# Where the moving operands of a two-block transformer step start: inner activations moved to byte 192 of 256, other inputs to byte 128

## The chip, the cores and the metric

The program runs on one core of a Trainium2 chip, in one launch. The metric is the device time in microseconds, the median of several runs.

## The reference

256 tokens of 1024 features, with 256 tokens of context, go through two blocks of two layers each. All matrices are fp32.

- First block, for each of two layers: a half feed-forward, an attention (differential in the first layer, grouped with norms of queries and keys in the second) and another half feed-forward. Each has a modulated norm ahead of it, `rmsnorm(h) * (1 + scale) + shift`, and joins the stream as `h + gate * rmsnorm(y)`. A feed-forward is `(silu(x Wg) * (x Wu)) Wout`, 1024 to 2816 to 1024. The context's stream goes along until the second layer's attention; the last feed-forward has the 256 tokens alone.
- Second block, for each of two layers: one wide projection of `rmsnorm(x)` feeds a sparse attention over 64 chosen keys, a stick-breaking attention and a matrix memory. Each of the three results is gated, projected by `w_branch` and weighted by a sigmoid of further columns of the projection. Their sum goes through `w_out` onto the stream. A last norm ends the program.

## The kernel before

**Products.** Features lie on the 128 partitions and tokens along the free axis: 512 tokens (latent and context) or 256. An fp32 value is kept as two exact parts, high and low, of type fp32r. `unit` makes the parts of a weight tile, `wh` on ScalarE (L60) and `wl` on VectorE (L61), from a raw tile that `load` (L52) brings over SP's queue. `mm3` (L75) does three products for one k-tile of 128 features: `wh` with the input's high part (L78), `wh` with its low part (L79), `wl` with its high part (L80). In each the weights (128 columns) are the stationary operand, and the input is the moving one, 512 or 256 columns wide. TensorE runs them one behind the other in the program's order, and loads the next weights while a product runs.

**Inputs.** A sublayer's input x has 8 tiles of high parts, `xh0` to `xh7`, and 8 of low parts, from `new_x` (L265). In a feed-forward `psg` holds the products of `w_in` with x. The inner activations are split into `gh` and `gl` (L320, L321), tiles of the pool `slot`, and `psy` holds the products of `w_out` with them (`wout`, L347). With a `done` and two halves of tokens, the last pass of `wout` takes its last four columns one half of the tokens after the other, 256 wide. The attentions keep their outputs for `wout` in `slot` too (`oh`, `ol`, `ohl`), as well as the grouped attention's keys (`gkh`, `gkl`). In the second block `pair` (L792) does two units of 128 columns into one bank `psp`, 256 wide, from x or from a branch's parts `bh`, `bl`.

**Places.** A pool's tiles are given addresses in the order in which the pools are opened (`run`, L1354). The weights' pool `w`, the constants, `h` and `tmp` stay through both blocks. In bytes from the start of a partition, as the allocator gives them out for the kernel before:

| pool | starts at | byte in 256 | holds |
|---|---|---|---|
| `w` | 51,648 | 192 | `wh`, `wl`, 512 bytes for a k-tile |
| `x` | 84,416 | 192 | `xh`, `xl` of the first block, 2,048 bytes each |
| `yq` | 117,184 | 192 | y, queries, keys |
| `slot` | 195,200 | 128 | 16 tiles of 2,048 bytes: `gh`, `gl`, `oh`, `ol`, `ohl`, `gkh`, `gkl` and others |
| `x2` | 128,672 | 160 | `xh`, `xl` of the second block, 1,024 bytes each |
| `y2` | 145,056 | 160 | the second block's other tiles of 512 columns, `bh` and `bl` among them |

A half of the tokens begins 1,024 bytes into its tile, and every tile here is a multiple of 256 bytes long, so all moving operands of a pool start at the same byte in 256.

**Order.** In the first block the steps that make the modulation's vectors (`psada`) and other small work are dealt out between the units. In the second block the attentions' steps and the projections that don't depend on them alternate. Loads wait on SP's queue until their raw tile is free: three raw tiles in the first block, two in the second. `w` holds four units.

Of the kernel before, what the change touches and what calls it, by code (L numbers as in the profile page):

```python
# [4 lines left out]
F32 = mybir.dt.float32  # L5
# [7 lines left out]
KC = 8  # L13
DFF = 2816
EPS = 1e-6
LAMBDA_INIT = 0.8 - 0.6
# Tiles of one tag take their slots in the order of the program: streams that may overtake each other have tags of their own.
PSUM_TAGS = ({"p": 2, "s": 2, "a": 2, "o": 1, "f": 1}, {"p": 2, "s": 2, "a": 1, "b": 3})
PSUM_OF = {}         # name -> tags taken in turn, for the first and for the second block
# [13 lines left out]
# the other partition of a pair that is rotated: neighbours, and eight apart  # L33
# [10 lines left out]
class Block:  # L44
# [25 lines left out]
    def behind(self, ins, prev):  # L70
        """issue order alone: ins after prev on their engine"""
        self.tc.add_manual_dep(ins.ins, prev.ins.name,
                               mybir.DependencyInfo(mybir.DependencyClass.NoSync, mybir.DependencyReason.DATA), reason="order")
# [8 lines left out]
    def split(self, hi, lo, src):  # L82
        """src (SBUF or PSUM, fp32) -> hi, lo"""
        self.nc.scalar.copy(hi, src)
        self.nc.vector.tensor_sub(lo, src, hi.bitcast(F32))

# [1 line left out]
    def setup(self):  # L88
# [7 lines left out]
        # condition vectors, silu; a stationary block of 32 columns for each k-tile begins with its two  # L96
# [11 lines left out]
        # rows of 128 features -> columns  # L108
# [11 lines left out]
    def vecs(self, aps, name):  # L120
        """list of [r, 128] DRAM rows -> one [128, sum r] SBUF tile"""
# [19 lines left out]
    def adaln(self, i, blocks, tiles="adaw", ahead=2):  # L141
        """blocks of 512 columns of the modulation, evenly spaced, as a list of steps; a step's loads come ahead of its products"""
# [3 lines left out]
        nm = 4 // nj            # k-tiles in a step: four products side by side in the array's columns  # L146
# [46 lines left out]
    def gtab(self, i, kind, k, out=None, cs=slice(0, 8)):  # L193
        """per-feature scale tables, [128, 8, 2]"""
# [13 lines left out]
    def rstd_rows(self, acc, n=256, mean=1.0 / D):  # L208
        """acc [128, n]: partial sums of squares over partitions -> 1/rms on every partition, in PSUM [128, n]"""
# [11 lines left out]
    def spread(self, rs):  # L221
        """columns of token scalars -> one row on every partition, in PSUM"""
# [8 lines left out]
    def sumsq(self, src_of, hf, tag, eng=None, pin=False):  # L231
        """sum over chunks of src^2 (SBUF) for a half -> acc [128, 256]"""
# [14 lines left out]
    def pre_norm(self, hf, G, mT, k, R=None):  # L247
        """x = split(rmsnorm(h) * G + B), this half"""
# [16 lines left out]
    def new_x(self, n=512):  # L265
        self.xh = [self.xp.tile([128, n], F32R, name=f"xh{c}", tag=f"xh{c}") for c in range(KC)]
        self.xl = [self.xp.tile([128, n], F32R, name=f"xl{c}", tag=f"xl{c}") for c in range(KC)]
# [5 lines left out]
    def ffn_units(self, i, f, c):  # L273
        """gate and up columns c, then those of c + 1"""
        w = self.I['ffn_w_in'][i, f]
        raws = [self.load(w[:, o + c * 128:o + c * 128 + 256], 8, 256) for o in (0, DFF)]
        return [self.unit(raw, 8, j * 128) for j in range(2) for raw in raws]

    def ffn(self, i, f, halves, done, fill=(), then=None, mid=None):
# [3 lines left out]
        if len(halves) == 2:  # L283
            self.new_y()
        else:
            self.y = self.h[1]      # the context's stream has ended
        # places for the fill: after each pair of w_in units, after each pair of w_out columns of all but the last pass
        self.set_fill(fill, DFF // 128 + 4 * (len(PASSES) - 1))
        for pi, (p0, p1) in enumerate(PASSES):
            nk = p1 - p0  # L290
            gh, gl = {}, {}
            for c in range(p0, p1, 2):
# [5 lines left out]
                if c == 0:  # L298
                    for hf, s in [(0, slice(0, width))] if mid else [(hf, HALF[hf]) for hf in halves]:
                        if hf:  # L300
                            self.step_tail(9)
                        # the last chunks unit by unit: the first units give up their place sooner
# [7 lines left out]
                for j in range(2):  # L310
# [9 lines left out]
                    a = self.sp.tile([128, 512], F32R, name="gh", tag="slot")  # L320
                    b = self.sp.tile([128, 512], F32R, name="gl", tag="slot")  # L321
# [10 lines left out]
    def warm(self, func):  # L332
        """have the table of a function loaded before it is needed"""
# [3 lines left out]
    def place(self):  # L337
        """a place in the program for steps of other work"""
# [8 lines left out]
    def wout(self, w, oh, ol, halves, first, done=None):  # L347
        """y (+)= w^T o; with done, the last columns come for one half of the tokens after the other"""
# [64 lines left out]
    def proj(self, ps, w, xs, sls, nk=8):  # L413
        """ps[:, sl] = w^T x[:, sl] for each slice, k inner"""
# [17 lines left out]
    def rope(self, x, n, other, cs):  # L432
        """x [128, n*256] in SBUF, rotated in place; cs [128, 2, 256]"""
# [15 lines left out]
    def rsqrt(self, ss, n, mean, name, eps=EPS):  # L449
        """(ss * mean + eps) ** -0.5 for a few columns"""  # L450
# [8 lines left out]
    def da(self, done):  # L459
# [10 lines left out]
        # -lambda on every partition  # L470
# [22 lines left out]
        def front(h):  # L493
            """projections of one head, in steps"""
# [52 lines left out]
    def da_qk(self, ps, name, scale, cs, out):  # L547
        """q or k of a head: rotated where the tokens are latent ones, split; the rotation is left to the caller's moment"""
# [12 lines left out]
    def vtok(self, vT, v):  # L561
        """v^T -> v with tokens on partitions, [128, 4*128]"""
# [63 lines left out]
    def ga(self, done):  # L626
# [15 lines left out]
        def q_pair(ps):  # L642
            """two heads: gain, rotation, split; 1 / rms apart"""
# [7 lines left out]
            def rest():  # L651
# [3 lines left out]
                rq = self.rsqrt(pss[:, 0:4], 4, 1.0, "q", 128.0 * EPS)      # with the scores' 128 ** -0.5  # L655
# [4 lines left out]
        # queries first: the context's half of x is still on its way  # L660
# [22 lines left out]
        # keys and values of all tokens  # L683
# [108 lines left out]
    def pair(self, raw, nk=8, x=None, c0=0):  # L792
        """two 128-column units of raw -> one bank [128, 2*256]"""
# [8 lines left out]
    def silu_gate(self, ps, name):  # L802
        """2 * silu(ps)"""
# [13 lines left out]
    def small_units(self, l):  # L817
        """weights of the narrow projections in two units, spread over the rows where they are needed;
        what the other rows of the product hold is of no use, but their columns are there"""
# [8 lines left out]
    def hybrid(self, l):  # L828
# [4 lines left out]
        # projections that the sparse attention needs first  # L833
# [74 lines left out]
        # up-projections of the keys, transposed, 16 zero rows in front of each head  # L908
# [11 lines left out]
        for cp in range(2):  # L920
            qa = {}
            ps = [self.pst("psqa") for e in range(2)]      # the two halves of the rows write different banks
# [9 lines left out]
            ol = [self.t2("olat") for c in range(2)]       # heads 4cp, 4cp+1 | 4cp+2, 4cp+3  # L932
# [65 lines left out]
        accs = self.hc          # the context's stream has ended  # L998
# [40 lines left out]
    def index_bias(self, t, iq, ik, iw, sc):  # L1039
        """0 where a key is among the 64 chosen for the query, -1e30 elsewhere"""  # L1040
# [23 lines left out]
    def tok_rows(self, src, dst_of, n=2):  # L1064
        """two banks of [128 features x 2, 256 tokens] -> tokens on partitions; src: list of SBUF tiles [128, 512]"""
# [67 lines left out]
    def ml_proj(self, l, qk, va):  # L1133
        """projections for the matrix memory, as a list of steps"""
# [29 lines left out]
    def mlstm(self, l, ig, fg, qk, va, more):  # L1164
        nc = self.nc
        # gates, one head on each of four partitions
# [7 lines left out]
        nc.vector.scalar_tensor_tensor(ex, fg, 0.0, ex, ALU.min, ALU.subtract)      # log sigmoid(f)  # L1174
# [64 lines left out]
    def final(self):  # L1239
        """out = h g / rms(h), tokens on partitions: there 1 / rms is a scalar of each partition"""  # L1240
# [51 lines left out]
    def low(self, xl, t, B, xh):  # L1292
        """t + B less its high part; t is spent."""
# [3 lines left out]
    def first_block(self):  # L1297
# [3 lines left out]
        # the first shift and scale come in two parts, and the first products need only the first of them  # L1301
# [26 lines left out]
        def steep(i, g):  # L1328
            """the first steps of a group wait for the boundary"""
# [24 lines left out]
    def run(self):  # L1354
        tc, nc, I = self.tc, self.nc, self.I
        from contextlib import ExitStack
        with ExitStack() as es:
# [6 lines left out]
            with ExitStack() as e1:  # L1364
# [6 lines left out]
                self.gp = pool("gt", 3, e1)  # L1371
                self.sp = pool("slot", 16, e1)
                self.setup()
                self.first_block()
            with ExitStack() as e2:
# [4 lines left out]
                self.small = pool("small", 1, e2)  # L1380
                self.xp = pool("x2", 1, e2)
# [48 lines left out]
class Join:  # L1430
    """A sublayer's output y joins the stream, h' = h + G y / rms(y), and the next sublayer's input follows from it,
    x = h' G' / rms(h') + B, for one half of the tokens at a time.
    Both means of squares are ready together: sum h'^2 = sum h^2 + 2 r sum h G y + r^2 sum (G y)^2, r = 1 / rms(y).
    post, pre: (layer, first modulation chunk)"""
# [18 lines left out]
    def stream(self):  # L1453
        """sum of h^2"""
# [7 lines left out]
    def chunk(self, hf, c):  # L1462
        """sums over the chunks of features of y^2, h G y and (G y)^2, tokens along the free axis"""
# [12 lines left out]
        if c == KC - 1:  # L1476
            b.hold = (last, add, 4, 4)      # the fourth of the next units of weights comes behind

    def finish(self, hf):
        """in parts: other products come between them"""  # L1480
# [134 lines left out]
```

## Time and profile before

| | |
|---|---|
| median of 3 runs | 2602.63 us (2601.14 to 2602.85) |
| span of the profiled execution, first to last instruction | 2598.3 us |
| median less that span | 4.3 us |
| TensorE busy | 2500.7 us (96%) |
| mean granted clock of TensorE | 0.984 of full |
| VectorE, ScalarE, GpSimd busy | 55%, 40%, 16% |

The profiled execution has no time of its own besides its span. In the profile PE is TensorE, PEld its loading of weights, DVE VectorE, ACT ScalarE, POOL GpSimd and SP the engine whose queue issues most transfers. A product is listed with its start and a duration that reaches past the start of the next, so the distance between starts is not the duration. A name is that of a tile in the program; L78 is line 78.

### The profile page before, as it was taken

The page shows a single profiled execution, that of the slowest core. Times are in us where ns is not written, and L with a number is a line of the kernel's source. Part 1 is how long each engine was busy: PE and PEld are TensorE (multiplying, and loading weights), DVE is VectorE, ACT ScalarE, POOL GpSimd, SP SyncE. Part 2 cuts the span into 40 slices and gives each one's busy share as a digit, 9 for nine tenths or more (in the row PEclk, how much of TensorE's full clock was granted, in tenths as well). Part 3 has the DMA queues.
Part 4 walks back from the last instruction along what each step waited for, and adds up shares of the span by engine and source line. Part 5 has one row for each costly group of instructions (what it writes and reads, how often), then busy time and mean ns, then how long its engine had stood idle before and what let it go on. Part 6 is the DMA issues. An engine that isn't in the chain of part 4 may idle for free. (4 is left out here: it accounts for less than half of the span.)

```text
span 2598.3 us, 38082 instructions
## 1 busy us (share of the span) xinstructions
PE 2500.7 (96%) x15175; PEld 2105.4 (81%) x15175; DVE 1435.2 (55%) x2492; ACT 1038.1 (40%) x1740; POOL 406.3 (16%) x427
## 2 busy tenths in 40 slices
PE   7999999999999999999999999999989999899998
PEld 3777778666678888788888887799887999788998
DVE  4333337666565333474333477656785765676755
ACT  3222234554353222343222355644444544446443
POOL 1000016220051000150000153400330010201010
PEclk9999998999999999999999999999999999999999
DMA  8443423344432322243332243455533356433453
GB/s 282 153 154 129 147 97 99 126 148 150 149 116 86 107 97 97 98 146 114 114 101 94 98 155 125 143 182 180 161 105 113 106 158 194 140 98 114 138 187 130
DMA packets 321789, 346.56 MB, mean 133 GB/s; under 512 B 23906, under 2 KB 282568, under 8 KB 321612
## 3 DMA queue, kind: packets, MB, share of 16 engines
q1 hardware_dynamic: 320706, 343.35, 40.9%
q8 instruction: 119, 1.95, 0.3%
q10 hardware_dynamic: 906, 0.78, 0.1%
q14 instruction: 58, 0.48, 0.1%
HBM read 343.04 MB, written 1.05 MB: 132 GB/s over the span
## 5 line engine op out<-in xcount | busy, mean ns | idle before, releaser
L60 ACT CAST wh<-raw 128x1024 fp32r<-128x1024 f32 (+2 forms) x534 | 527.8, 998 | 1120.7 <-PE psg L79 554.1
L61 DVE TENSOR_TENSOR wl<-raw,wh 128x1024 fp32r<-128x1024 f32 (+2 forms) x534 | 639.4, 1203 | 549.0 <-ACT wh L60 547.0
L79 PE MATMUL psg<-xl,wh 128*128 128x512 f32 (+1 forms) x1472 | 523.6, 356 | 3.1 <-POOL xl L1295 3.0
L78 PE MATMUL psg<-xh,wh 128*128 128x512 f32 (+1 forms) x1472 | 523.3, 357 | 2.9 <-ACT xh L1322 2.3
L80 PE MATMUL psg<-xh,wl 128*128 128x512 f32 (+1 forms) x1472 | 521.4, 355 | 0.0
L78 PE MATMUL psp<-xh,wh 128*128 128x256 f32 x1248 | 357.2, 287 | 10.0 <-DVE mlu L1156 3.8
L80 PE MATMUL psp<-xh,wl 128*128 128x256 f32 x1248 | 354.5, 284 | 3.1 <-DVE wl L61 3.1
L79 PE MATMUL psp<-xl,wh 128*128 128x256 f32 x1248 | 356.7, 286 | 0.6 <-POOL xl L855 0.6
L78 PEld LDWEIGHTS psg<-xh,wh 128*128 128x128 f32 x1472 | 277.3, 189 | 59.0 <-ACT wh L60 12.6
L79 PEld LDWEIGHTS psg<-xl,wh 128*128 128x128 f32 x1472 | 278.2, 189 | 53.1 <-issue 8.1
L80 PEld LDWEIGHTS psg<-xh,wl 128*128 128x128 f32 x1472 | 278.0, 189 | 39.7 <-issue 0.8
L79 PE MATMUL psy<-gl,wh 128*128 128x512 f32 (+1 forms) x800 | 273.8, 342 | 2.6 <-DVE gl L323 2.5
L78 PE MATMUL psy<-gh,wh 128*128 128x512 f32 (+1 forms) x800 | 275.2, 344 | 0.0
L80 PE MATMUL psy<-gh,wl 128*128 128x512 f32 (+1 forms) x800 | 273.6, 342 | 0.0
L78 PEld LDWEIGHTS psp<-xh,wh 128*128 128x128 f32 x1248 | 237.3, 190 | 16.3 <-issue 5.7
L80 PEld LDWEIGHTS psp<-xh,wl 128*128 128x128 f32 x1248 | 237.6, 191 | 5.4 <-DVE wl L61 4.1
L79 PEld LDWEIGHTS psp<-xl,wh 128*128 128x128 f32 x1248 | 237.9, 191 | 4.1 <-issue 2.4
L243 POOL TENSOR_TENSOR acc<-acc,sq 128x256 f32<-128x256 f32 x70 | 56.9, 816 | 1108.2 <-ACT acc L237 1102.5
L319 DVE TENSOR_TENSOR g<-sg,psg 128x512 f32<-128x512 f32 (+1 forms) x88 | 54.5, 620 | 223.4 <-PE psg L80 223.4
L78 PEld LDWEIGHTS psy<-gh,wh 128*128 128x128 f32 x800 | 150.3, 188 | 26.4 <-ACT wh L60 5.0
L79 PEld LDWEIGHTS psy<-gl,wh 128*128 128x128 f32 x800 | 151.1, 189 | 22.7 <-DVE gl L323 3.2
L80 PEld LDWEIGHTS psy<-gh,wl 128*128 128x128 f32 x800 | 150.5, 188 | 21.6 <-issue 1.7
(473 smaller groups left out, 3651.6 us busy)
## 6 DMA issues: line engine op xcount, KB each, us to landing
raw<-in_ffn_w_in SPq DMA_DIRECT2D x88, 1024.0 KB
raw<-in_w_in SPq DMA_DIRECT2D x70, 1024.0 KB
adaw<-in_ada_w SPq DMA_DIRECT2D x240, 256.0 KB
raw<-in_ffn_w_out SPq DMA_DIRECT2D x32, 1024.0 KB
adas<-in_ada_w SPq DMA_DIRECT2D x48, 256.0 KB
raw<-in_ffn_w_out SPq DMA_DIRECT2D x16, 768.0 KB
raw<-in_da_w_in SPq DMA_DIRECT2D x12, 1024.0 KB
raw<-in_w_branch SPq DMA_DIRECT2D x24, 512.0 KB
```

The costliest lines, as they stand in the source:

```text
L60: a = nc.scalar.copy(wh[:, 0:nk, :], r)
L61: b = nc.vector.tensor_sub(wl[:, 0:nk, :], r, wh[:, 0:nk, :].bitcast(F32))
L78: mm(ps, lhsT=wh[:, k, :], rhs=xh, start=first, stop=False)
L79: mm(ps, lhsT=wh[:, k, :], rhs=xl, start=False, stop=False)
L80: mm(ps, lhsT=wl[:, k, :], rhs=xh, start=False, stop=last)
L243: b = (eng or nc.vector).tensor_tensor(acc, acc, sq, ALU.add)
L319: nc.vector.tensor_mul(g[:, 0:width], sg[:, 0:width], pu[:, 0:width])
```

## The change

Four edits move tiles within their partition. No instruction, transfer or wait is added or taken away. Comments and docstrings are gone too.

```diff
-    def new_x(self, n=512):
-        self.xh = [self.xp.tile([128, n], F32R, name=f"xh{c}", tag=f"xh{c}") for c in range(KC)]
-        self.xl = [self.xp.tile([128, n], F32R, name=f"xl{c}", tag=f"xl{c}") for c in range(KC)]
+    def new_x(self, n=512, at=0):
+        self.xh = [self.xp.tile([128, at + n], F32R, name=f"xh{c}", tag=f"xh{c}")[:, at:at + n] for c in range(KC)]
+        self.xl = [self.xp.tile([128, at + n], F32R, name=f"xl{c}", tag=f"xl{c}")[:, at:at + n] for c in range(KC)]
...
-                    a = self.sp.tile([128, 512], F32R, name="gh", tag="slot")
-                    b = self.sp.tile([128, 512], F32R, name="gl", tag="slot")
+                    at = 0 if width == 512 else 48
+                    a = self.sp.tile([128, 512], F32R, name="gh", tag="slot")[:, at:at + width]
+                    b = self.sp.tile([128, 512], F32R, name="gl", tag="slot")[:, at:at + width]
...
                 self.gp = pool("gt", 3, e1)
+                pool("pad", 1, e1).tile([128, 16], F32, name="pad")
                 self.sp = pool("slot", 16, e1)
...
                 self.small = pool("small", 1, e2)
+                pool("pad2", 1, e2).tile([128, 56], F32, name="pad2")
                 self.xp = pool("x2", 1, e2)
...
         if not self.ready:
-            b.new_x()
+            if len(self.hacc) == 1:
+                b.new_x(256, 48)
+            else:
+                b.new_x()
             self.ready = True
```

Worked out from the table of places:

- `pad` is 64 bytes, so `slot` starts at 195,264, byte 192 of 256, with all that lies in it.
- In the last feed-forward, the only one that is 256 wide, `gh` and `gl` start 48 elements, 192 bytes, into their tile: byte 128, as before.
- The join ahead of the last feed-forward is the only one with one half of the tokens that makes a new x. That x starts 192 bytes into its tile, at 84,608: byte 128 in place of 192.
- `pad2` is 224 bytes, so `x2` starts at 128,896 and `y2` at 145,280: byte 128 in place of 160.
- `w`, `x` for the other sublayers, and `yq` stay where they are.

## Rows read from the trace of the kernel before

**Rows 1.** The page: span, and busy time by engine.
```profile
span 2598.3 us, 38082 instructions
...
PE 2500.7 (96%) x15175; PEld 2105.4 (81%) x15175; DVE 1435.2 (55%) x2492; ACT 1038.1 (40%) x1740; POOL 406.3 (16%) x427
```

**Rows 2.** Stages: us, busy PE PEld DVE ACT POOL, clock, DMA share, GB/s.
```profile
1130.00:1505.00 375.00, 374.84 (x1810) 304.59 (x1808) 162.87 (x238) 115.74 (x175) 44.97 (x51) 1.00 0.34 112
1683.00:1886.00 203.00, 193.72 (x1609) 192.40 (x1609) 132.53 (x204) 94.47 (x140) 32.21 (x32) 0.97 0.53 167
1886.00:2240.00 354.00, 337.99 (x2595) 313.16 (x2595) 236.93 (x431) 170.85 (x262) 43.71 (x51) 0.99 0.46 138
2240.00:2598.00 358.00, 339.64 (x2602) 314.99 (x2601) 232.26 (x425) 166.08 (x258) 40.52 (x46) 0.98 0.41 133
```

**Rows 3.** TensorE's groups by shape: busy us, mean ns | idle before.
```profile
L78 PE MATMUL psg<-xh,wh 128*128 128x512 f32 x992 | 388.4, 392 | 2.3 <-ACT xh L1322 2.3
...
L78 PE MATMUL psp<-xh,wh 128*128 128x256 f32 x1248 | 357.2, 287 | 10.0 <-DVE mlu L1156 3.8 <-ACT xh L854 3.6 <-ACT wh L60 0.8
...
L78 PE MATMUL psy<-gh,wh 128*128 128x512 f32 x432 | 171.5, 397 | 0.0
...
L78 PE MATMUL psg<-xh,wh 128*128 128x256 f32 x480 | 134.9, 285 | 0.6 <-ACT xh L1514 0.6
L78 PE MATMUL psy<-gh,wh 128*128 128x256 f32 x368 | 103.6, 282 | 0.0
...
L78 PE MATMUL psp<-bh,wh 128*128 128x256 f32 x192 | 54.1, 282 | 0.0
```

**Rows 4.** TensorE in order of time, 512 wide, input xh: start us, us.
```profile
1271.62 0.39 PE L80 MATMUL psg<-xh,wl 128*128 128x512 f32 x1
...
1311.99 0.39 PE L78 MATMUL psg<-xh,wh 128*128 128x512 f32 x1
```

**Rows 5.** The same, 512 wide, input gh, second feed-forward.
```profile
961.83 0.39 PE L78 MATMUL psy<-gh,wh 128*128 128x512 f32 x1
...
1003.83 0.39 PE L78 MATMUL psy<-gh,wh 128*128 128x512 f32 x1
```

**Rows 6.** The same, 256 wide, input xh, last feed-forward.
```profile
1739.73 0.28 PE L78 MATMUL psg<-xh,wh 128*128 128x256 f32 x1
...
1759.89 0.28 PE L78 MATMUL psg<-xh,wh 128*128 128x256 f32 x1
```

**Rows 7.** The same, 256 wide, input gh, last feed-forward.
```profile
1782.78 0.28 PE L80 MATMUL psy<-gh,wl 128*128 128x256 f32 x1
...
1802.95 0.28 PE L78 MATMUL psy<-gh,wh 128*128 128x256 f32 x1
```

**Rows 8.** The same, 256 wide, input gh, after another product came between.
```profile
1860.59 0.50 PE L1458 MATMUL psst<-ones,acc 128*128 128x1 f32 x4
...
1861.15 0.28 PE L79 MATMUL psy<-gl,wh 128*128 128x256 f32 x1
...
1872.22 0.28 PE L80 MATMUL psy<-gh,wl 128*128 128x256 f32 x1
```

**Rows 9.** The same, 256 wide, second block.
```profile
2109.84 0.28 PE L79 MATMUL psp<-xl,wh 128*128 128x256 f32 x1
...
2131.96 0.28 PE L80 MATMUL psp<-bh,wl 128*128 128x256 f32 x1
```

**Rows 10.** SP's queue in order of time, second block's loads: start us, us.
```profile
2123.50 0.37 SPq L52 DMA_DIRECT2D raw<-in_w_in  x1
...
2141.56 18.40 SPq L52 DMA_DIRECT2D raw<-in_w_in  x5
```

**Rows 11.** What ScalarE waited for from 2100 to 2240: us, times, longest.
```profile
ACT wh L60 <- DMA raw<-in_w_in: 36.8, 11, 6.1
ACT wh L60 <- PE psp L79: 17.2, 14, 2.2
```

**Rows 12.** What TensorE waited for in the second block: us, times, longest.
```profile
PE psR L228 <- DVE dg L227: 3.9, 3, 1.9
```

## The prediction

> **What bounds the kernel now.** I read the page first, then the stages, then TensorE's groups by shape, and last TensorE's instructions in order of time. The page gives TensorE 2500.7 us of a span of 2598.3 us, VectorE 55% and ScalarE 40% [rows 1]. The stages say the same of each place that the change touches: TensorE is busy 374.84 of 375 us in the third feed-forward, 193.72 of 203 us in the last one, and 338 to 340 of some 356 us in each layer of the second block [rows 2]. In the second block its longest single cause of waiting sums to 3.9 us [rows 12]. So the time is the number of products times their pitch, the distance from one start to the next. A mean duration doesn't show it, since products overlap (392 ns long, 227 ns apart). I take the pitch from the first and the last of a list of consecutive products.
>
> - 512 wide, input `xh` at byte 192: 179 rows, 40.37 us over 178 steps, 226.8 ns [rows 4].
> - 512 wide, input `gh` at byte 128: 181 rows, 42.00 us over 180 steps, 233.3 ns [rows 5].
> - 256 wide, `xh` at 192: 169 rows, 20.16 us over 168 steps, 120.0 ns [rows 6].
> - 256 wide, `gh` at 128: 179 rows, 20.17 us over 178 steps, 113.3 ns [rows 7].
> - The same tiles at the same addresses later in the same stage, after products of another kind came between: 95 rows, 11.07 us over 94 steps, 117.8 ns [rows 8]. Byte 128 therefore has two steady pitches, and which one a chain falls into is set where it starts.
> - 256 wide, second block at byte 160: 188 rows, 22.12 us over 187 steps, 118.3 ns [rows 9].
>
> The weights lie at byte 192 in all six. What the reader is to see is that width and byte together go with the pitch: 512 wide is quicker at 192 than at 128, 256 wide quicker at 128 than at 192. The trace holds only these pairs.
>
> **The change part by part.** No instruction is added or removed, and no transfer. The two pads are never written, so they cost nothing. Every tile behind a pad moves, and so do the engines' accesses to it. VectorE's and ScalarE's part in that I cost at zero: their work lies beside TensorE's 96%, and no row shows either of them at two addresses. Without that cover a per cent on VectorE would be 14 us of its 1435 us [rows 1].
>
> *Inner activations, 512 wide, 128 to 192.* There are 3 x 432 = 1,296 such products [rows 3]. If they take the pitch of `xh` at the same byte, each gains 233.3 − 226.8 = 6.5 ns: 8.4 us. The 96 products of the differential attention's output (8 k-tiles, 4 columns of weights, 3 products) lie in the same pool and give 0.6 us more. Together −9.0 us. The bounds are 0, if the byte is not what counts, and −9.0.
>
> *256-wide products that come along to 192.* The first three feed-forwards and the differential attention do their last four columns one half after the other: 4 columns x 2 halves x 8 k-tiles x 3 = 192 products each, 768 in all. The grouped attention's output adds 8 x 8 x 3 = 192. These 960 go from 117.8 or 113.3 ns to 120.0. I take 2.2 ns each, the gap from the pitch that follows an interruption, as they do: +2.1 us; the other end is +6.4 us.
>
> *The last feed-forward's input, 192 to 128.* Its 44 columns of weights x 8 x 3 are 1,056 of the 3 x 480 products [rows 3]. At 113.3 ns they gain 6.7 ns each, 7.1 us; at 117.8 they gain 2.3 us, and the 528 `gh` products behind them, which mostly run at 113.3 now, would stay in the slower pitch too and give back up to 1.9 us, so the low end is −0.4. I take −7.1, because the nearest row is the same stage, width, byte and weights, and there 113.3 holds through whole passes [rows 7]. The `gh` tiles of this stage end at byte 128 as before, and cost nothing.
>
> *The second block's input, 160 to 128.* There are 3 x (1,248 + 192) = 4,320 products [rows 3]. At 128 each gains between 0.5 ns (117.8) and 5.0 ns (113.3). Here the chains are interrupted often by attention work and I have no row that says into which pitch they fall, so I take the middle, 2.8 ns: 12.1 us. Not all of it reaches the end. Where a gate's load and a branch's load alternate, the loads set their own pace: two rounds take 2141.56 − 2123.50 = 18.06 us on SP's queue, 9.03 us each [rows 10], while their 48 + 24 products need only 72 x 118.3 ns = 8.52 us; ScalarE waited 36.8 us for these transfers and 17.2 us for TensorE [rows 11]. A quicker product only waits sooner there. I count four stretches of some 30 us (two a layer), 1,000 products, and the first 20 to 25 us of each layer, some 300, where the splits of the weights arrive just in time. That leaves 3,000 products: −8.4 us, with bounds −1.5 and −15.
>
> The chip's notes speak against this change. The Trainium skill (TensorE: Matmul & The Clock Gate, section Part 2: What happens when you issue a matmul) says that TensorE reads the moving operand and the weights through two independent ports, so that loading the next weights takes nothing from the running product. By that rule the byte of a tile would matter to neither, every part above would be zero, and the time would stay. The trace doesn't agree as far as it goes: equal widths have pitches of 113.3 to 120.0 ns [rows 6, 7].
>
> Sum: −9.0 + 2.1 − 7.1 − 8.4 = −22.4 us on a span of 2598.3 us, 2575.9 us. The runs' median, 2602.63, is 4.3 us above this span; I add that, and predict **2580 us**.
>
> **The rivals.**
> - *The quick pitch nowhere.* What is late next is the chain after an interruption: the 117.8 ns of [rows 8] holds in the last feed-forward and the second block. For it: the change is seen there at the very address that is wanted. Against it: whole passes at 113.3. Then −9.0 + 2.1 − 0.4 − 1.5 = −8.8: 2594 us.
> - *The quick pitch everywhere.* −9.0 + 2.1 − 7.1 − 15 = −29: 2574 us, or 2567 us if the loads keep up as well and all 4,320 products gain 5.0 ns.
> - *It changes nothing.* The pitch belongs to the stage (how long its chains are, who empties PSUM), and the bytes only go along with it, since each stage has one address. For it: six pairs, and no stage at two addresses. Against it: `psg` and `psy` are alike in all but their tiles, yet the sign of their difference turns over with the width. 2603 us. The Trainium skill's rule on the two ports (TensorE: Matmul & The Clock Gate, Part 2) ends at this time too.
> - *Slower.* Byte in 256 is not the right measure. In 512 the weights and `xh` lie at 448 alike; `gh` would come to 192 and the second block's input to 384, pairs that no row shows, while the last feed-forward's input comes to 128, where `gh` is now. If the new 512-wide pair costs as much beyond 233.3 as 226.8 lies below it (+9.0 us), and the second block takes 120.0 ns (+7.3 us), the last feed-forward's 7.1 us don't pay for it: +9.2, 2612 us. It decides once these two cost more than 7.1 us together.
>
> **How the numbers follow.** Chances: the forecast 0.55 (its own range 2573 to 2588, from a little more or less of the middle pitch and of the waits), the quick pitch nowhere 0.2, everywhere 0.12, nothing 0.08, slower 0.05. About 0.2%, 5 us, is what a measurement of this kernel can tell from no change. Faster by more than that: 0.55 + 0.2 + 0.12, less 0.01 for small gains, 0.86. Within it: 0.09. Slower: 0.05. For 8 in 10 the range takes in the quick pitch everywhere below and the quick pitch nowhere above, with 4 us for its waits: 2566 to 2598 us. It leaves out "nothing" and "slower".
>
> **What would show it.** Pitches, read as above: `psy` 512 wide at 227 ns, the split halves at 120, the last feed-forward's `psg` at 113 or 118, the second block's `psp` anywhere from 113 to 118. The third feed-forward's stage should shorten by some 2.5 us, the last one by 7 us. In the rounds of gate and branch, ScalarE should wait longer for transfers and TensorE more for weights, with the round on SP's queue still near 9.0 us. I am wrong if `psy` 512 wide stays at 233, if `psg` of the last feed-forward is at 120 at its new byte, or if the second block's products are quicker and its layers take as long as before.

## The result, and the profile after

The changed kernel takes 2579.8 us (median of 4 runs, 2579.08 to 2580.62) beside 2601.89 us before (2600.38 to 2602.85). The ratio is 0.9915, 95% interval 0.9901 to 0.9929. Faster, as predicted, and 0.2 us from the number; the interval is some 7 us wide, so the 0.2 says little.

The page of the changed kernel, beside [rows 1]. The span is 20.9 us shorter, TensorE's busy time 29.5 us less, with the same instructions; VectorE and ScalarE are as busy as before:

```profile
span 2577.4 us, 38082 instructions
...
PE 2471.2 (96%) x15175; PEld 2085.2 (81%) x15175; DVE 1438.2 (56%) x2492; ACT 1038.4 (40%) x1740; POOL 406.0 (16%) x427
```

TensorE in order of time after the change, as in [rows 4 to 9]; each pair is the first and the last row of a list without a gap:

```profile
959.73 0.39 PE L79 MATMUL psy<-gl,wh 128*128 128x512 f32 x1
...
1001.44 0.39 PE L80 MATMUL psy<-gh,wl 128*128 128x512 f32 x1
...
1115.77 0.28 PE L78 MATMUL psy<-gh,wh 128*128 128x256 f32 x1
...
1127.89 0.28 PE L80 MATMUL psy<-gh,wl 128*128 128x256 f32 x1
...
1688.78 0.28 PE L79 MATMUL psg<-xl,wh 128*128 128x256 f32 x1
...
1709.98 0.28 PE L79 MATMUL psg<-xl,wh 128*128 128x256 f32 x1
...
1727.73 0.28 PE L79 MATMUL psg<-xl,wh 128*128 128x256 f32 x1
...
1749.94 0.28 PE L80 MATMUL psg<-xh,wl 128*128 128x256 f32 x1
...
2101.74 0.28 PE L80 MATMUL psp<-xh,wl 128*128 128x256 f32 x1
...
2123.95 0.28 PE L78 MATMUL psp<-bh,wh 128*128 128x256 f32 x1
...
2135.76 0.28 PE L79 MATMUL psp<-xl,wh 128*128 128x256 f32 x1
...
2157.90 0.28 PE L78 MATMUL psp<-xh,wh 128*128 128x256 f32 x1
```

- `psy` 512 wide at byte 192: 41.71 us over 184 steps, 226.7 ns, for 233.3 in [rows 5].
- The split halves at 192: 12.12 us over 101 steps, 120.0 ns.
- The last feed-forward's `psg` at 128, first pass over `w_in`: 21.20 us over 180 steps, 117.8 ns; second pass: 22.21 us over 196 steps, 113.3 ns, for 120.0 in [rows 6]. The third pass is like the second.
- The second block at 128: 113.3 ns (196 steps in 22.21 us) and twelve microseconds later, behind a wait that is shown below, 117.8 ns (188 steps in 22.14 us), for 118.3 in [rows 9].

The 12,744 products of `mm3` in the traces (L78 to L80) stand in the same order in both kernels, so the start of each can be compared. The start before less the start after, at the edges of the stages (worked out from both traces):

```
place                                     start before   gain up to there, us
first product                                  34.6       -0.9
first feed-forward, w_out, 3 passes           114.4       gains 0.9 + 1.2 + 0.6
third feed-forward, w_out, 3 passes          1225.4       gains 0.9 + 1.2 + 0.6
grouped attention begins                     1532.9        7.7
last feed-forward begins                     1683.3        9.2
  after its first pass over w_in             1719.1        8.5
  before and after its second               1735.8        8.5, then 11.1
  before and after its third                1803.6       11.1, then 13.6
second block begins                          1885.8       14.3
last projection                              2588.6       20.9
```

Around 1680 us two of these differences go with the clock and not with the pitch. The join ahead of the last feed-forward takes 14.81 us before and 12.78 after, a gain of 2.0 us without any product of `mm3` in it. TensorE's granted clock stood at its lower level (1.2 of 2.4 GHz) from 1673.7 to 1680.5 in the trace of before, inside the join, and from 1675.7 to 1679.1 in that of the changed kernel, inside the first pass over `w_in`. There some 15 products more than before take 213 ns, and the pass as a whole loses 0.7 us although its pitch fell.

The next two answers show where the second block gives something back. First ScalarE and TensorE around 2131 to 2135 us of the changed kernel; in brackets the idle time before an instruction and what ended it:

```profile
2131.58 2.00 ACT L60 CAST wh<-raw 128x1024 fp32r<-128x1024 f32 x2 [5.65 <-DMA raw<-in_w_in]
2133.49 0.58 ACT L986 ACTIVATE mg<-psp 128x512 f32<-128x512 f32 x1
```

```profile
2133.12 0.28 PE L80 MATMUL psp<-bh,wl 128*128 128x256 f32 x1
2134.12 0.39 PE L78 MATMUL psp<-xh,wh 128*128 128x256 f32 x1 [0.73 <-ACT mg L986]
```

ScalarE stands 5.65 us behind a late load. The step that empties a PSUM bank (`mg`) is queued behind the two splits of that load, and TensorE waits 0.73 us for the bank. The products had a pitch of 113.3 ns up to this wait; behind it they run at 117.8.

TensorE's waits behind `mg` over the whole second block (us, times, longest), before and then after:

```profile
PE psp L78 <- ACT mg L985: 0.7, 1, 0.7
PE psp L78 <- DVE mg L1021: 0.7, 1, 0.7
```

```profile
PE psp L78 <- ACT mg L986: 3.9, 6, 1.0
PE psp L78 <- DVE mg L1022: 1.7, 2, 0.9
```

And the loads on SP's queue after the change, as in [rows 10]; two rounds take 2125.88 − 2107.68 = 18.20 us, 9.10 each:

```profile
2107.68 0.37 SPq L52 DMA_DIRECT2D raw<-in_w_in  x1
...
2116.76 0.37 SPq L52 DMA_DIRECT2D raw<-in_w_in  x1
...
2125.88 2.17 SPq L52 DMA_DIRECT2D raw<-in_w_in  x2
```

The queue's round is not TensorE's. TensorE's goes from the first product of one branch to that of the next; first three rounds of the kernel before, then two and one of the changed kernel:

```profile
2121.08 0.28 PE L78 MATMUL psp<-bh,wh 128*128 128x256 f32 x1
...
2146.64 0.28 PE L78 MATMUL psp<-bh,wh 128*128 128x256 f32 x1
```

```profile
2105.26 0.28 PE L78 MATMUL psp<-bh,wh 128*128 128x256 f32 x1
...
2121.57 0.28 PE L78 MATMUL psp<-bh,wh 128*128 128x256 f32 x1
...
2130.51 0.28 PE L78 MATMUL psp<-bh,wh 128*128 128x256 f32 x1
```

Before, TensorE makes them in 25.56 us, 8.52 each, without a wait: the loads lag, but do not hold it yet. After the change two rounds take 8.16 us and the third 8.94, with a wait behind `mg` of 0.50 us in it. The four stretches of three rounds in the two layers take 103.2 us before and 102.8 after (worked out from the traces): in the rounds hardly anything was gained.

### The profile page after: what moved, and what is told of

It is laid out like the page before. It is cut to its first block, busy times and chain, and to the rows that moved or that the text cites. A ratio compares the mean times of both kernels' runs of the same rounds, so it can differ in the third digit from the quotient of the medians.

```text
span 2577.4 us, 38082 instructions
## 1 busy us (share of the span) xinstructions
PE 2471.2 (96%) x15175; PEld 2085.2 (81%) x15175; DVE 1438.2 (56%) x2492; ACT 1038.4 (40%) x1740; POOL 406.0 (16%) x427
## 4 chain that ended last, share of the span: by engine, by line
PE 72%; issue 11%; DVE 9%; POOL 4%; ACT 3%; DMA 2%; SPq 0%; DVEq 0%; POOLq 0%; ACTq 0%
PE psg L79 11%; PE psg L78 11%; PE psg L80 11%; PE psy L78 6%; PE psy L79 6%; PE psy L80 5%; PE psada L164 3%; DVE wl L61 3%; PE psp L79 3%; PE psp L78 3%; PE psp L80 3%; ACT wh L60 1%; DMA raw<-in_w_in 1%; PE pso L607 1%; PE psk L78 1%
## 5 line engine op out<-in xcount | busy, mean ns | idle before, releaser
L78 PE MATMUL psg<-xh,wh 128*128 128x512 f32 (+1 forms) x1472 | 521.3, 356 | 2.9 <-ACT xh L1323 2.3
L80 PE MATMUL psg<-xh,wl 128*128 128x512 f32 (+1 forms) x1472 | 520.6, 354 | 0.0
L78 PE MATMUL psp<-xh,wh 128*128 128x256 f32 x1248 | 352.8, 283 | 13.6 <-DVE mlu L1157 4.2
L80 PE MATMUL psp<-xh,wl 128*128 128x256 f32 x1248 | 349.9, 281 | 3.4 <-DVE wl L61 3.3
L78 PEld LDWEIGHTS psg<-xh,wh 128*128 128x128 f32 x1472 | 276.3, 188 | 59.0 <-ACT wh L60 12.6
L80 PEld LDWEIGHTS psg<-xh,wl 128*128 128x128 f32 x1472 | 277.9, 189 | 39.8 <-issue 0.8
L78 PE MATMUL psy<-gh,wh 128*128 128x512 f32 (+1 forms) x800 | 272.9, 341 | 0.0
L80 PE MATMUL psy<-gh,wl 128*128 128x512 f32 (+1 forms) x800 | 271.3, 339 | 0.0
L78 PEld LDWEIGHTS psp<-xh,wh 128*128 128x128 f32 x1248 | 235.6, 189 | 20.9 <-issue 5.7
L80 PEld LDWEIGHTS psp<-xh,wl 128*128 128x128 f32 x1248 | 236.1, 189 | 6.0 <-DVE wl L61 4.7
L78 PEld LDWEIGHTS psy<-gh,wh 128*128 128x128 f32 x800 | 150.8, 189 | 23.3 <-ACT wh L60 5.0
L80 PEld LDWEIGHTS psy<-gh,wl 128*128 128x128 f32 x800 | 150.9, 189 | 18.7 <-issue 1.7
```

Source lines behind the costliest of these rows:

```text
L78: mm(ps, lhsT=wh[:, k, :], rhs=xh, start=first, stop=False)
L80: mm(ps, lhsT=wl[:, k, :], rhs=xh, start=False, stop=last)
```

## The experiments

Theories. *Distance*: the pitch goes with the distance of the input's byte from the weights' byte, modulo 256, and with the width. *Own byte*: the input's byte in 256 counts, whatever the weights'. *Stage*: the pitch belongs to the stage and the bytes only go along. And on what the second block gave back: *loads* or *attention steps*.

**One part at a time.** The inner activations alone:

```diff
+                pool("pad", 1, e1).tile([128, 16], F32, name="pad")     # gh, gl of the last feed-forward at 48
```

> Only `slot` moves, to byte 192; the last feed-forward's gh and gl stay at 128 and its input at 192, the second block at 160. By the prediction -9.0 + 2.1 = -6.9 us against before (ratio 0.9973), psy 512 wide at 226.8 ns, the split halves and the grouped attention's output at 120.0 ns; the other end of the second term would leave -2.6 us. If the pitch belongs to the stage: 0 us, psy 512 wide at 233.3 ns. From the trace of the whole change, stage by stage, I read a gain of 8.4 to 9.6 us for this part (some 1.2 us of it differ at the program's start, ahead of any moved tile).

Measured: 2594.74 us beside 2601.81 before, ratio 0.9968 (0.9956 to 0.9981), −7.1 us by the medians. `psy` 512 wide runs at 226.7 ns (183 steps in 41.48 us) in the same stage that showed 233.3 [rows 5]:

```profile
959.64 0.39 PE L79 MATMUL psy<-gl,wh 128*128 128x512 f32 x1
...
1001.12 0.39 PE L79 MATMUL psy<-gl,wh 128*128 128x512 f32 x1
```

This rules *stage* out. The last feed-forward's input alone:

```diff
-            b.new_x()
+            b.new_x(256, 48)                                             # where one half of the tokens is left
```

> Only the last feed-forward's input moves, from byte 192 to 128. By the prediction -7.1 us (ratio 0.9973), all of its products at 113.3 ns. From the trace of the whole change, -5.1 us (0.9980), since there the first pass over w_in ran at 117.8 ns. If the 528 gh products fall into 117.8 ns with it: -0.4 us (0.9998).

Measured: 2594.46 us, 0.9970 (0.9957 to 0.9982), −7.4 us. TensorE in its profiled execution, first and second pass over `w_in`:

```profile
1696.80 0.28 PE L78 MATMUL psg<-xh,wh 128*128 128x256 f32 x1
...
1716.99 0.28 PE L79 MATMUL psg<-xl,wh 128*128 128x256 f32 x1
...
1736.78 0.28 PE L80 MATMUL psg<-xh,wl 128*128 128x256 f32 x1
...
1758.92 0.28 PE L79 MATMUL psg<-xl,wh 128*128 128x256 f32 x1
```

113.4 ns (178 steps in 20.19 us), then 117.8 (188 steps in 22.14 us), and the third pass at 117.8 too: the reverse of what the changed kernel shows at the same addresses. That execution took 2599.22 us, the slowest of its six (2592.68 to 2599.22); the six lie 2.6 to 9.1 us under the kernel before, as far apart as the prediction's two ends for this part (0.4 and 7.1 us). So the choice between the two pitches is not made by the addresses of the two operands and the order of the products alone. The second block alone:

```diff
+                pool("pad2", 1, e2).tile([128, 56], F32, name="pad2")
```

> Only the second block's x2 and y2 move, from byte 160 to 128. By the prediction -8.4 us (ratio 0.9968); from the trace of the whole change -6.6 us (0.9975), some 3.3 us of which look like fewer products at the lower of the clock's two levels and not like pitch; by the quick pitch nowhere, -1.5 us (0.9994). If the first block's shift in time doesn't matter to it, the three parts run alone sum to the whole (-22 us) within 2 us.

Measured: 2595.31 us, 0.9975 (0.9966 to 0.9984), −6.5 us. The three ratios leave 0.32, 0.30 and 0.25%, 0.87% together, beside 0.85% for the whole change: the parts add, within their intervals.

**Weights moved too.**

```diff
+            pool("pad0", 1).tile([128, 16], F32, name="pad0")
             self.wp = pool("w", 4)
```

> The changed kernel with 64 bytes more ahead of the weights' pool: weights at byte 0, 512 wide inputs at 0, last feed-forward's inputs and second block at 192 (the split halves at 0). If the distance from the weights' byte counts, every pitch is as in the changed kernel (226.8; 113.3 or 117.8; split halves 120.0) and the time is 2580 us. If the input's own byte counts, whatever the weights': the second block's 4,320 and the last feed-forward's 1,584 products, 256 wide at 192, take 120.0 ns as 256 wide at 192 did before, some 5 us slower in the last feed-forward than before and 10 to 20 us slower in the second block than the changed kernel: about 2600 us or more, and the 512 wide at byte 0 are a pair that no row shows.

Measured: 2575.34 us, 0.9897 (0.9883 to 0.9910). TensorE, 512 wide at byte 0; last feed-forward at byte 192, first and second pass; second block at byte 192:

```profile
954.61 0.39 PE L80 MATMUL psy<-gh,wl 128*128 128x512 f32 x1
...
996.77 0.39 PE L80 MATMUL psy<-gh,wl 128*128 128x512 f32 x1
...
1685.80 0.28 PE L79 MATMUL psg<-xl,wh 128*128 128x256 f32 x1
...
1705.97 0.28 PE L80 MATMUL psg<-xh,wl 128*128 128x256 f32 x1
...
1739.81 0.28 PE L80 MATMUL psg<-xh,wl 128*128 128x256 f32 x1
...
1761.95 0.28 PE L79 MATMUL psg<-xl,wh 128*128 128x256 f32 x1
...
2089.79 0.28 PE L79 MATMUL psp<-xl,wh 128*128 128x256 f32 x1
...
2111.94 0.28 PE L78 MATMUL psp<-xh,wh 128*128 128x256 f32 x1
```

226.7 ns (186 steps in 42.16 us), 113.3 (178 in 20.17), 117.8 (188 in 22.14) and 117.8 (188 in 22.15). At byte 192 beside weights at 192 the same last feed-forward showed 120.0 [rows 6]; beside weights at 0 it shows the pair that belonged to 128 beside 192. *Distance* holds, *own byte* falls. All tiles behind the weights' pool moved along here, and no run moved the weights alone; that the weights are the partner is argued from their being the other operand that TensorE reads. The 4.5 us below the changed kernel were not expected; the two intervals overlap, and their cause stays open.

The opposite sign, with the second block brought to the weights' own byte:

```diff
+                pool("pad2", 1, e2).tile([128, 8], F32, name="pad2")
```

> The kernel before with the second block at byte 192, distance 0 from the weights, and nothing else moved. If the distance sets the pitch, the second block's products run at 120.0 ns, 1.7 ns slower than before over some 4,200: 7.1 us of products. Where they wait for other work anyway some of it is taken from the waits: I expect 3 to 7 us slower than before (ratio 1.0012 to 1.0027). If its own byte and not the distance counts, the same pitch here, so this run doesn't tell those two apart; if the gain of the part alone came from the clock and from waits and not from the pitch, 0 us.

Measured: 2603.57 us, 1.0009 (1.0001 to 1.0018), +2.6 us. Its products run at 120.0 ns (184 steps in 22.08 us, first and last row below), so the pitch did what was expected; the time lies just under the range I gave.

```profile
2461.83 0.28 PE L80 MATMUL psp<-bh,wl 128*128 128x256 f32 x1
...
2483.91 0.28 PE L78 MATMUL psp<-xh,wh 128*128 128x256 f32 x1
```

**A sweep of bytes.**

```diff
-                pool("pad", 1, e1).tile([128, 16], F32, name="pad")
+                pool("pad", 1, e1).tile([128, 32], F32, name="pad")      # second kernel: 48
-                    at = 0 if width == 512 else 48
+                    at = 0 if width == 512 else (8, 16, 24)[pi]          # second kernel: (36, 44, 12)
-                pool("pad2", 1, e2).tile([128, 56], F32, name="pad2")
+                pool("pad2", 1, e2).tile([128, 24], F32, name="pad2")    # second kernel: 40
-                b.new_x(256, 48)
+                b.new_x(256, 8)                                          # second kernel: 16
```

> A sweep, for pitches and not for the time; weights stay at byte 192. `slot` goes to byte 0, the last feed-forward's input to 224, its gh and gl to 32, 64 and 96 in its three passes, the second block to byte 0. That is 512 wide at a distance of 64 ahead of the weights' byte (in 256), and 256 wide at 32, 96, 128, 160 and 64. If the distance counts and grows or shrinks the pitch evenly, 512 wide lies between 226.7 and 233.4 ns and every 256 wide one between 113.4 and 120.0; if only a common byte is special (distance 0: 226.7 to 226.9 and 120.0), all others show 233.3 at 512 wide and 113.4 or 117.8 at 256 wide; 118.3 at 224, which before shows, speaks against the second.

> The same sweep at other bytes: `slot` at 64 (distance 128), the last feed-forward's input at 0 (distance 64), its gh and gl at 208, 240 and 112 (distances 16, 48 and 176), the second block at 64 (distance 128). Even change with the distance: pitches between those of 0 and 192. Only a common byte special: 233.3 at 512 wide, 113.4 or 117.8 at 256 wide. Were a 256 wide distance to show one pitch alone at or under 113.4, it would beat the changed kernel in the second block and the last feed-forward.

One run each: 2586.58 and 2598.91 us. Pitches of all kernels, each from the first and last row of a list without a gap, by distance (input's byte less weights' byte, modulo 256):

```
distance    512 wide, ns       256 wide, ns
   0        226.7, 226.9       120.0
  16                           118.7
  32                           116.7 and 117.8
  48                           118.3
  64        228.9              113.3 and 117.8
  96                           120.0
 128        233.3              118.6 and 120.0
 160                           117.3 and 118.6
 176                           119.3
 192        233.3              113.3 and 117.8
 224                           118.3
```

Two of these lists, 512 wide at 64 and 256 wide at 96 (184 steps in 42.11 us, 110 in 13.20):

```profile
957.66 0.39 PE L79 MATMUL psy<-gl,wh 128*128 128x512 f32 x1
...
999.77 0.39 PE L80 MATMUL psy<-gh,wl 128*128 128x512 f32 x1
```

```profile
1713.79 0.28 PE L80 MATMUL psy<-gh,wl 128*128 128x256 f32 x1
...
1726.99 0.28 PE L79 MATMUL psy<-gl,wh 128*128 128x256 f32 x1
```

Neither expectation holds: the change with the distance is not even, and a common byte is not the only special one. Of the bytes tried, the change uses the best ones: distance 0 at 512 wide, and at 256 wide one of the two distances (64 and 192) that reach 113.3. None has 113.3 alone. Modulo 512 the distances 0, 64 and 192 each hold two: `xh` 512 wide lies at the weights' byte and `gh` of the changed kernel 256 from it, both at 226.7 to 226.9 ns. So 256 and not 512 is the measure.

**What took the rest of the second block's gain.** Half of each load of eight k-tiles, used twice (the weights of k-tiles 4 to 7 are those of 0 to 3):

```diff
-        self.nc.sync.dma_start(raw[:, 0:nk, 0:cols], src.rearrange("(k p) c -> p k c", p=128))
+        self.nc.sync.dma_start(raw[:, 0:4, 0:cols], src[0:512].rearrange("(k p) c -> p k c", p=128))
...
+            r = raw[:, 0:4, c0:c0 + cols].unsqueeze(1).to_broadcast([128, 2, 4, cols])
```

> The kernel before, with half the bytes of each load of eight k-tiles in the second block: the first four k-tiles alone, used for k-tiles four to seven again (products, splits and their order are the same). If loads hold the second block up where gate and branch alternate, it is some 3 to 8 us faster than before; if they lie beside other work, within 1 us of it.

> The same halved loads with the second block at byte 128. The part alone gained 6.5 us, with a pitch that fell by 4.0 ns over 4,320 products (17 us): some 10 us were given back in waits. If loads took them, the gain over the kernel with halved loads at byte 160 is 12 to 17 us; by the prediction's split (1,000 products in rounds that loads pace, 300 at the layers' starts) it grows by two or three us, to 9; if the waits belong to the attentions' steps on the other engines, it stays at 6.5 us.

Measured: 2602.08 us (1.0008, 0.9999 to 1.0017) and 2592.52 us (0.9975, 0.9966 to 0.9985). Between the two lie 9.6 us by the medians, by the ratios 0.33%, 8.6 us: more than 6.5 and below 12, but too uncertain to tell the expectations apart. The first run shows no gain: by the medians it is 2.3 us slower, though its interval still holds the "within 1 us". The shorter loads also changed the program's order (689 of TensorE's 15,175 places in the trace differ from before), so only the pair can be compared, not either with the kernel before.

A raw tile of their own for the branch loads, with its own turn:

```diff
-        raw = self.rawp.tile([128, 8, 256], F32, name="raw", tag="raw")
+        if self.phase and nk == 4:
+            raw = self.rawp.tile([128, 4, 256], F32, name="rawb", tag="rawb", bufs=1)
+        else:
+            raw = self.rawp.tile([128, 8, 256], F32, name="raw", tag="raw")
```

> The kernel before, with a raw tile of 4 KB of its own for the branch loads (four k-tiles) beside the two of 8 KB in the second block; x2 and y2 stay at byte 160. TensorE waited only 0.7 us there behind a ScalarE step that stands behind a late load (mg), so: 0 to -2 us against before (ratio 0.9992 to 1.0).

> The changed kernel with the same third raw tile. If what the second block gives back in the rounds of gate and branch is late loads (TensorE's waits behind mg grew from 0.7 to 5.6 us, and none were left with halved loads), those waits go and it is 3 to 5 us faster than the changed kernel: about 2575 us, ratio 0.990 to before. If the transfers themselves are too slow for the quicker products, and not the turn of the raw tiles, it stays at 2580 us.

> The kernel with everything 64 bytes on (weights at 0) and the third raw tile. The distances are those of the changed kernel, so it should take the time of rb_after within 2 us, and less than both kernels of this case.

Measured: 2594.70 us (0.9976, 0.9966 to 0.9985), 2575.11 us (2569.71 to 2583.46; 0.9904, 0.9887 to 0.9920) and 2573.53 us (0.9894, 0.9881 to 0.9907). The first is a miss: −6.3 us where I expected 2 at most (and the waits behind `mg` in the kernel before were 1.4 us, not 0.7). The second is where it was expected, but its interval overlaps with that of the changed kernel; the third is within 2 us of it. Here, too, some of TensorE's places change (200 of 15,175), and loads on SP's queue move ahead, so what the tile and what the order gave is not told apart. The rounds of gate and branch on SP's queue, in the changed kernel with the third tile and in the one with everything 64 bytes on:

```profile
2116.75 0.37 SPq L55 DMA_DIRECT2D raw<-in_w_in  x1
...
2125.23 0.37 SPq L55 DMA_DIRECT2D raw<-in_w_in  x1
```

```profile
2116.82 0.37 SPq L55 DMA_DIRECT2D raw<-in_w_in  x1
...
2124.98 0.37 SPq L55 DMA_DIRECT2D raw<-in_w_in  x1
```

8.48 and 8.16 us, that is 72 products at 117.8 and at 113.3 ns, for 9.03 [rows 10] and 9.10. With a third tile the queue's round is as long as TensorE's products, and the two kernels' profiled executions happen to stand in different pitches. TensorE has no wait behind `mg` left in either.

The second block by kind of step, worked out from the profiled execution of each kernel, from its first projection's product to its last: steps from one projection's product to the next of under 140 ns; of 140 to 235 ns while the clock stood at its lower level of 1.2 GHz (nearly all 213 or 214 ns); of 140 to 235 ns at the full clock; longer ones; and the stretches that hold attention's products. The kernels by name: x2_at192 and e3_second have the second block alone moved, to 192 and 128; e4_all64 is the changed kernel with everything 64 bytes on; hl_ are the two with halved loads, at 160 and at 128; rb_ are the three with the third raw tile.

```
kernel         whole     under 140 ns        lower clock   full clock   longer   with attention
               us        mean ns   us        steps   us    us           us       us
before         702.7     118.30    492.4     67      14.2  22.9         15.9     157.4
x2_at192       705.8     119.83    502.0     42       9.0  23.0         15.9     155.9
changed        696.1     114.99    481.1     35       7.5  24.4         20.7     162.4
e3_second      696.1     114.37    477.1     46       9.8  24.2         21.4     163.6
e4_all64       693.8     116.08    486.7     39       8.2  22.5         15.5     160.8
hl_before      703.9     118.30    493.9     55      11.6  22.0         12.4     163.9
hl_second      695.9     115.49    481.9     55      11.7  22.2         13.1     167.0
rb_before      696.9     118.29    496.4     47       9.9  21.2         10.9     158.4
rb_after       692.8     116.29    489.0     38       8.0  21.5         10.8     163.5
rb_all64       686.3     114.28    478.0     60      12.7  21.4         11.7     162.5
```

With before's loads the longer steps grow by 4.8 and 5.5 us when the pitch falls (before to changed and to e3_second); with halved loads by 0.7, and with the third raw tile by −0.1 and 0.8. So the loads took that part of what was given back, shown by the waits though not by the medians alone. In e4_all64, whose rounds of gate and branch stood at 117.8 ns, the longer steps don't grow. The stretches with attention grow by 3 to 6 us wherever the pitch falls, whatever the loads, which speaks for *attention steps* as the other part; in the changed kernel and in e3_second 2.8 and 4.2 us more of them than before stand at the lower clock, which is some of it. Which step it is that waits there was not tested. The miss of rb_before shows here, too: its longer steps are 5.0 us less than before's, and those that are gone were waits behind `mg`, `wl` and `wh` near the end of each layer's branches (from 2199 to 2212 and from 2562 to 2567). That fits loads that have fallen behind by then, but the order of TensorE's products changed there as well.

## Why the prediction was right

**Inner activations, −9.0 + 2.1.** The mechanism is right: alone it gave −7.1 us for −6.9. In the trace the first and the third feed-forward gain some 2.7 us each in their `w_out` passes, for 432 x 6.5 ns = 2.8. The second gains 3.9 us, 1.0 of it from 3.4 us at the lower clock that only the kernel before had there. The split halves do run at 120.0.

**Last feed-forward's input, −7.1.** Right in the mean (−7.4 alone), but I took 113.3 ns for all 1,056 products from [rows 7], and the pitch is chosen anew behind each interruption: the changed kernel has the 768 of its second and third pass at 113.3, and of the 288 of its first pass the last 189 at 117.8. Its table of gains shows 2.5 + 2.5 us in the two passes; what the first gained by its pitch went to the steps at the lower clock.

**Second block, −8.4.** Right within 2 us (−6.5 alone, 6.6 in the trace), by sizes that were off against each other. The middle pitch was to gain 2.8 ns; measured are 3.3 (changed) and 3.9 (alone), 2.2 in e4_all64, so a mean over the chains is a fair guess and no single execution keeps to it. The step that was mis-sized is "not all of it reaches the end": I took 3.6 us (1,300 products x 2.8 ns). In the changed kernel 3.3 ns over some 4,180 products are 13.8 us, and the longer steps and the attention's stretches gave back 9.8, 4.8 of it behind late loads. There 32 fewer steps at the lower clock, some 97 ns each, gave 3.1 us; in e3_second 21 fewer gave 2.0. I put all of the absorption down to loads and to the layers' starts, and left out the stretches with attention. I also took the queue's 9.03 us for the pace of the round: most of TensorE's own rounds were 8.52 us, and in the first rounds of a layer loads held it only once these had become 8.16.

**The number.** That the sum came within 0.2 us is partly luck. In the two traces the gain up to the grouped attention is 8.6 us for 7.3 foretold (−9.0 and 768 x 2.2 ns), the join ahead of the last feed-forward adds 2.0 us that have no term, the last feed-forward gives 5.1 for 7.1 and the second block 6.6 for 8.4.

**The round on SP's queue near 9.0 us** is as foretold: 9.10. TensorE did not wait more for weights, as I had written (4.5 us before behind `wh` and `wl`, 3.9 after, over the second block), but for PSUM banks behind `mg`. That ScalarE waits longer for transfers shows over the block, not in every stretch: 73.8 us before and 88.7 after for `w_in`.

```profile
ACT wh L60 <- DMA raw<-in_w_in: 73.8, 25, 6.1
```

```profile
ACT wh L60 <- DMA raw<-in_w_in: 88.7, 26, 5.7
```

**The third and the last feed-forward** were to shorten by 2.5 and 7 us: 2.7 in the third's passes of `w_out`, 5.1 in the last one, where the two quick passes gave 2.5 each.

**The rivals.** *It changes nothing* falls with the run of the inner activations alone: moving tiles changed 233.3 to 226.7 ns, and moving the weights with them kept the pitches. With it falls, for this kernel, what the prediction drew from the Trainium skill's rule of two independent read ports (TensorE: Matmul & The Clock Gate, Part 2: What happens when you issue a matmul), that a tile's byte matters to neither. That it is the two ports that meet here is not shown. *Slower* falls too: the changed kernel's 512 wide pair, 256 apart in 512, has the low pitch. *Quick pitch nowhere* and *everywhere* are both half true, chain by chain.

## What to carry to other kernels

Where TensorE runs fp32r products without a gap, compare the start-to-start distance by the input's byte less the weights' byte modulo 256, for each width apart; one look with several bytes maps it. Then ask of each stage whether TensorE sets its pace: the rounds of gate and branch gave hardly anything for their quicker pitch (103.2 us before, 102.8 after), while a raw tile of 4 KB, with the order that came with it, gave 6.3 us, as much as the whole move of the second block's input. The two together, with everything 64 bytes on, took 2573.53 us, 1.06% under the kernel before; below the changed kernel by 0.21%, which the two intervals don't tell from nothing.

## What the runs showed of the hardware that was not expected

- At distances 64 and 192 a chain of 256 wide products keeps one of two pitches, 113.3 or 117.8 ns, until it is interrupted; in rb_after two lists of over 900 products held 117.8, in rb_all64 two held 113.3 throughout. What picks one stayed open: the same address took either in different kernels' executions, and within one ([rows 7] and [rows 8]). In the traces of eight kernels no chain at these distances changed its pitch without a step of over 135 ns in between. Between them lie 4.4 ns, 26 us over the 5,900 products of the last feed-forward and the second block, which would be enough for the 13.8 us between the runs of rb_after; that this is their cause was not shown, since only one execution of each kernel was profiled.
- The same byte of the input can have another pitch beside weights at another byte: 256 wide at byte 192 takes 120.0 ns beside weights at 192 and 113.3 or 117.8 beside weights at 0.
